# Finding and fetching the tokens of a rank one rank further ahead, ahead of the second product

## The chip, the cores and the metric

The kernel runs on one core of a Trainium2 chip. The metric is the device time of one execution in microseconds (us), as the median of several runs. Engines are named as the profile names them: PE (TensorE, matmuls and transposes; PEld is its weight load), DVE (VectorE), ACT (ScalarE), POOL (GpSimd, which also issues the indirect DMAs), SP (SyncE, which issues the weight loads).

## The reference, cut to what matters

One layer of a trunk for 512 prompt tokens and 8 sample tokens (520 rows, width 1024). After attention, a state space branch and a first layer norm comes a mixture of 64 experts, 8 for each token; this part is what the change touches.

```python
scores = sigmoid(xf @ w_router)
_, top_idx = top_k(scores + router_bias, 8)
gates = top_s / sum(top_s) * 2.5
# for every expert e, over the tokens tok that chose it, with gate g:
xb = x_pad[tok]
h = silu(xb @ w1[e]) * (xb @ w3[e])          # 1024 -> 256, twice
acc = acc.at[tok].add((h @ w2[e]) * g)       # 256 -> 1024
# and a shared expert for all tokens, then a second layer norm
```

## The kernel before, in words

The first 440 us compute everything up to the router. There the experts are sorted by how many tokens chose them; the position in this order is called the rank, 0 to 63, and rank e has a fixed capacity `CAPS[e]` (112 rows for the first, 56 for the last). Then the loop of `second_phase` (L1602) goes over the ranks. What one rank needs, by the names of the functions:

- `find(e)` (L1383): five small matmuls on PE (`x<-what,oh`) and three short DVE operations turn the one-hot table `oh` into the list of token numbers, `idx`, and the gates. PE writes into the one bank `x` (pool `psx`), which the side work uses too.
- `gather(e)` (L1412): POOL issues an indirect DMA that reads the listed rows of `xD` in memory into `XG[e % 3]`. There are three such buffers (`xg0` to `xg2`), so a gather must wait until the rank three before it has been turned.
- `turn(e)` (L1418): eight PE transposes of `xg` (`a<-ident,xg`), then ACT and DVE split the result into a high and a low part, `xgh` and `xgl`.
- `expert_in(e)`: the first product, 24 matmuls of 512 columns (`a<-hi,xgh`, `a<-lo,xgh`, `a<-hi,xgl`), over four chunks of weights; `ffn_mid` makes `hg` of it (ACT, DVE), and `ffn_turn(e)` transposes `hg` on PE and splits it into `hh` and `hl`.
- `expert_out(e)`: the second product, 12 matmuls (`mm<-hi,hh` and so on) over two chunks of weights; ACT scales it by the gate into `y`, and POOL issues a scatter, an indirect DMA that adds the rows of `y` to `accD` in memory.

The weights stream in the order of their use: for rank e+1 the four chunks of its first product, then the two chunks of the second product of rank e. Each chunk (512 KB) is loaded by SP into one of 7 raw buffers (5 more at the beginning), then split by ACT (`hi<-raw`) and DVE (`lo<-raw`) into one of 5 pairs of tiles; the `lo` of the first chunk of a second product is made by POOL, so POOL has, per rank, a gather, a scatter and one `lo`. Side work (the shared expert and the inputs of the layer, `x<-ph,...`) is spread over the ranks.

Step e of the loop issues: first product of e, turn of e+1, second product of e-1, `ffn_turn` of e, and then find and gather of e+3. This is the order in which the program is written; a scheduler then places the instructions of each engine, and may pull one ahead of others where it has its operands early by its own account. Each engine executes its instructions strictly in the placed order.

Of the kernel before, what the change touches and what calls it, by code (L numbers as in the profile page):

```python
# [31 lines left out]
NE = 64  # L32
# [168 lines left out]
def trunk_step(ctx: ExitStack, tc: tile.TileContext, I, O):  # L201
# [1074 lines left out]
    def shared_mid(out, hg):  # L1276
        S.activation(hg, out[:, 0:128], AF.Silu)
        mul(V, hg, hg, out[:, 128:256])
        return hg
# [128 lines left out]
    def fetch(e):  # L1408
        find(e)
        gather(e)  # L1410

    def gather(e):  # L1412
        m = CAPS[e]
        G.indirect_dma_start(out=XG[e % 3][0:m], out_offset=None, in_=xD[:, :],  # L1414
                             in_offset=bass.IndirectOffsetOnAxis(ap=IX[e][0:m, 0:1], axis=0),
                             bounds_check=NT - 1, oob_is_err=False)
# [60 lines left out]
    def second_phase():  # L1477
# [124 lines left out]
        for e in range(NE + 1):  # L1602
            if e == NE - 1:
                last_rows()
            if 0 < e < NE:
                expert_in(e)
            if 0 < e < NE - 1:
                turn(e + 1)
            if e:
                expert_out(e - 1)  # L1610
            else:
                H['shared'] = py.tile([128, 5, 2, 2, TT], F32R, tag="side", name="st")
                mids = py.tile([MAX_CAP, 1024], F32, tag="y", bufs=YB, name="mids")
                mids = [shared_mid(H['first half'][i], mids[0:TT, 128 * i:128 * i + 128]) for i in R5]
            if 0 < e < 6:
                shared_turn(mids[e - 1], e - 1, 0)
            if 0 < e < NE - 1:
                HT[e] = ffn_turn(HG.pop(e), CAPS[e])
            if e + 3 < NE:
                fetch(e + 3)  # L1620
            for i in {SECOND + 2: (0, 1, 2), SECOND + 3: (3, 4)}.get(e, ()):
                second_sums(i)
            if e == 4:
                close_pool(pre)
                pw = open_pool("pw")
            while side and (e - 4) * SIDE >= N_SIDE - len(side) + 1:
                q, i = side.pop(0)
                if q == -2:
                    shared_more(i)
                elif q == -1:  # L1630
                    shared_out(i)
                elif q < 4:
                    layer_inputs(q, i)
                else:
                    last_scales(i)
# [219 lines left out]
```

## Time and profile before

| | us |
|---|---|
| median of 3 runs (1320.13 to 1326.46) | 1321.36 |
| profiled execution, its own time | 1323.58 |
| its span, first to last instruction | 1321.8 |

The profile is one execution. The loop over the ranks fills it from about 440 to 1290 us. In the views used below a time is us from the start of the span; an idle time in brackets is how long the engine did nothing before that instruction, and what came last of what it waited for.

### The profile page before, as it was taken

What the parts mean: (1) busy time and instruction counts of PE and PEld (TensorE: products, weight loads), DVE (VectorE), ACT (ScalarE), POOL (GpSimd) and SP (SyncE); (2) the same over time, 40 slices, a digit from 0 to 9 for tenths busy, and PEclk for the clock granted to TensorE, in tenths of its full rate; (3) what the DMA queues carried; (4) which work ended last, traced back from release to release, by engine and by line L of the source; (5) the groups of instructions that cost most, each with busy time, mean ns of one, the idle gap of its engine ahead of it and who ended that gap; (6) DMA issues with size and microseconds to landing.
All of it is one profiled execution on the core that took longest, in us unless ns stands there. A gap on an engine that the chain in (4) does not pass through costs nothing. (4 is left out here: it accounts for less than half of the span.)

```text
span 1321.8 us, 20417 instructions
## 1 busy us (share of the span) xinstructions
PE 1182.6 (89%) x7082; PEld 884.3 (67%) x7084; DVE 933.0 (71%) x1440; ACT 702.9 (53%) x1055; POOL 459.2 (35%) x285
## 2 busy tenths in 40 slices
PE   6899999999997969888799888899899999988783
PEld 6899899899876846566566566677666666644341
DVE  7965658643487768576779666787878887766566
ACT  3232434233213656566567556677757767666463
POOL 1000000000012346343555335454555455465326
PEclk8899799999998879889999889999999999999897
DMA  9446553252523789889989978999999999979973
GB/s 367 158 135 167 198 162 129 72 155 83 180 77 106 246 217 274 254 263 304 296 254 314 290 237 278 285 329 314 321 311 313 335 314 299 303 249 289 260 230 97
DMA packets 112315, 312.92 MB, mean 237 GB/s; under 512 B 35121, under 2 KB 35545, under 8 KB 111135
## 3 DMA queue, kind: packets, MB, share of 16 engines
q1 hardware_dynamic: 78408, 261.74, 58.8%
q0 software_dynamic: 30848, 43.33, 14.8%
q10 hardware_dynamic: 2953, 6.52, 1.8%
q8 instruction: 57, 0.93, 0.3%
q14 instruction: 49, 0.40, 0.1%
HBM read 276.32 MB, written 32.87 MB: 234 GB/s over the span
## 5 line engine op out<-in xcount | busy, mean ns | idle before, releaser
L265 DVE TENSOR_TENSOR lo<-raw,hi 128x1024 fp32r<-128x1024 f32 x371 | 503.2, 1367 | 203.4 <-ACT hi L269 202.2
L269 ACT ACTIVATE hi<-raw 128x1024 fp32r<-128x1024 f32 x434 | 450.8, 1056 | 279.3 <-DMA raw<-in_we_dram 115.8
L210 PE MATMUL a<-hi,xgh 128*64 128x512 f32 (+18 forms) x512 | 212.3, 415 | 8.5 <-ACT hi L269 6.2
L1451 POOL DMA_INDIRECT accD<-y,idx x62 | 123.2, 1988 | 277.8 <-ACT hh L269 155.6
L210 PE MATMUL a<-lo,xgh 128*64 128x512 f32 (+18 forms) x512 | 210.9, 412 | 6.6 <-DVE lo L265 6.3
L210 PE MATMUL a<-hi,xgl 128*64 128x512 f32 (+18 forms) x512 | 207.0, 404 | 0.0
L265 POOL TENSOR_TENSOR lo<-raw,hi 128x1024 fp32r<-128x1024 f32 x63 | 168.3, 2672 | 62.5 <-ACT hi L269 51.8
L1414 POOL DMA_INDIRECT xg<-xD,idx x64 | 119.0, 1859 | 120.8 <-DVE idx L1396 57.9
L210 PE MATMUL mm<-xh,hi 128*128 128x260 f32 (+2 forms) x576 | 121.3, 292 | 16.6 <-ACT xh L269 6.6
L210 PE MATMUL mm<-xh,lo 128*128 128x260 f32 (+1 forms) x576 | 120.1, 290 | 1.8 <-DVE lo L265 1.8
L210 PE MATMUL mm<-xl,hi 128*128 128x260 f32 (+1 forms) x576 | 120.7, 291 | 0.8 <-DVE xl L265 0.8
L210 PEld LDWEIGHTS a<-hi,xgh 128*64 128x64 f32 (+18 forms) x512 | 75.7, 148 | 53.1 <-ACT hi L269 10.2
L210 PEld LDWEIGHTS a<-lo,xgh 128*64 128x64 f32 (+18 forms) x512 | 75.7, 148 | 45.4 <-DVE lo L265 10.7
L210 PEld LDWEIGHTS mm<-xh,hi 128*128 128x128 f32 x576 | 92.1, 195 | 17.5 <-ACT xh L269 6.3
L210 PEld LDWEIGHTS a<-hi,xgl 128*64 128x64 f32 (+18 forms) x512 | 75.7, 148 | 38.5 <-issue 4.3
L210 PE MATMUL mm<-lo,hh 128*64 128x512 f32 (+18 forms) x256 | 85.5, 416 | 12.8 <-POOL lo L265 9.9
L210 PEld LDWEIGHTS mm<-xh,lo 128*128 128x128 f32 x576 | 92.3, 195 | 2.1 <-DVE lo L265 2.0
L210 PEld LDWEIGHTS mm<-xl,hi 128*128 128x128 f32 x576 | 92.3, 195 | 1.5 <-DVE xl L265 1.1
L210 PE MATMUL mm<-hi,hh 128*64 128x512 f32 (+18 forms) x256 | 85.7, 417 | 8.0 <-ACT hi L269 7.6
L1450 ACT ACTIVATE y<-mm,both 78x1024 f32<-78x1024 f32 (+19 forms) x62 | 68.6, 1106 | 32.9 <-PE mm L210 29.8
L269 ACT ACTIVATE xgh<-a 128x256 fp32r<-128x256 f32 (+17 forms) x128 | 51.0, 408 | 63.7 <-PE a L215 63.0
L215 PEld LDWEIGHTS a<-ident,xg 64*128 64x128 f32 (+18 forms) x512 | 51.1, 147 | 48.9 <-issue 20.0
(410 smaller groups left out, 1919.4 us busy)
## 6 DMA issues: line engine op xcount, KB each, us to landing
raw<-in_we_dram SPq DMA_DIRECT2D x384, 512.0 KB
raw<-in_wd_dram SPq DMA_DIRECT2D x50, 512.0 KB
accD<-zeros_b POOLq DMA_DIRECT2D x2, 2560.0 KB, 23.7
praw<-in_wp_dram SPq DMA_DIRECT2D x8, 512.0 KB
base<-in_xtok_dram ACTq DMA_DIRECT2D x1, 2080.0 KB
xD<-base SPq DMA_DIRECT2D x5, 416.0 KB
base<-accD POOLq DMA_DIRECT2D x5, 416.0 KB, 22.8
acc<-accD SPq DMA_DIRECT2D x5, 416.0 KB
```

The costliest lines, as they stand in the source:

```text
L210: ins = nc.tensor.matmul(*a, **k)
L215: ins = nc.tensor.transpose(*a, **k)
L265: return e.tensor_tensor(out=o, in0=a, in1=b, op=ALU.subtract)
L269: a = S.activation(hi, src, AF.Copy)
L1414: G.indirect_dma_start(out=XG[e % 3][0:m], out_offset=None, in_=xD[:, :], in_offset=bass.IndirectOffsetOnAxis(ap=IX[e][0:m, 0:1], axis=0), ...
L1450: S.activation(y.rearrange("p (h n) -> p h n", h=2), ps[0:m], AF.Copy, scale=GC.pop(e)[0:m])
L1451: G.indirect_dma_start(out=sumsD[e % 2 if e < SECOND else 0][:, :], out_offset=bass.IndirectOffsetOnAxis(ap=IX.pop(e)[0:m, 0:1], axis=0), ...
```

## The change

In step e the find and the gather are now those of rank e+4 in place of e+3, and they stand between the turn of rank e+1 and the second product of rank e-1 in place of at the step's end. At step 0 ranks 3 and 4 are fetched together. The number of every kind of instruction stays the same; there are still three `XG` buffers, so the gather of rank e+4 goes into the buffer that the turn of rank e+1 has just read.

```diff
             if 0 < e < NE - 1:
                 turn(e + 1)
+            if e and e + 4 < NE:
+                fetch(e + 4)
             if e:
                 expert_out(e - 1)
...
             if 0 < e < NE - 1:
                 HT[e] = ffn_turn(HG.pop(e), CAPS[e])
-            if e + 3 < NE:
-                fetch(e + 3)
+            if e == 0:
+                fetch(3)
+                fetch(4)
```

Since the scheduler places instructions, the diff alone does not show where they come to stand. Three places follow.

POOL, around the gathers of ranks 15 to 17 (an `accD` row is a scatter, a `lo` row the split of a weight chunk, an `xg` row a gather). Before: gather 15, scatter 11, lo, scatter 12, lo, gather 16, gather 17, scatter 13.

```order
L1414 DMA xg0_4199<-xD_146,idx_6224 78x1024
L1451 DMA accD1_148<-y_6204,idx_5644 640x1024
L265 TENSOR_TENSOR lo_6287<-raw_6125,hi_6286 128x1024
L1451 DMA accD0_147<-y_6357,idx_5797 640x1024
L265 TENSOR_TENSOR lo_6408<-raw_6278,hi_6407 128x1024
L1414 DMA xg1_4201<-xD_146,idx_6377 78x1024
L1414 DMA xg2_4203<-xD_146,idx_6498 78x1024
L1451 DMA accD1_148<-y_6478,idx_5918 640x1024
```

Now, in the same engine and place: gather 15, scatter 10, lo, gather 16, scatter 11, lo, gather 17, scatter 12.

```order
L1414 DMA xg0_4199<-xD_146,idx_6051 78x1024
L1451 DMA accD0_147<-y_6081,idx_5340 640x1024
L265 TENSOR_TENSOR lo_6149<-raw_5987,hi_6148 128x1024
L1414 DMA xg1_4201<-xD_146,idx_6204 78x1024
L1451 DMA accD1_148<-y_6234,idx_5471 640x1024
L265 TENSOR_TENSOR lo_6302<-raw_6140,hi_6301 128x1024
L1414 DMA xg2_4203<-xD_146,idx_6357 78x1024
L1451 DMA accD0_147<-y_6387,idx_5624 640x1024
```

The gather of rank 16 has moved ahead of two scatters and two splits. From rank 9 on nearly every rank now has the pattern gather, scatter, lo, in which the gather of rank k stands just ahead of the scatter of rank k-5; before, the gathers of ranks 11, 12, 14 to 18, 40, 43, 44, 47 to 52 and 54 to 60 stood one or two scatters later than that, and most others there already. The gathers of ranks 23, 24, 25, 28 and 29 come to stand one scatter later than before.

POOL, at the beginning of the loop (scatter 0, lo, gather 4, then what follows).

```order
L1451 DMA accD0_147<-y_4724,idx_4298 640x1024
L265 TENSOR_TENSOR lo_4779<-raw_4467,hi_4778 128x1024
L1414 DMA xg1_4201<-xD_146,idx_4748 94x1024
L1451 DMA accD1_148<-y_4847,idx_4316 640x1024
L1414 DMA xg2_4203<-xD_146,idx_4871 92x1024
```

Those were the rows before; these are the rows now.

```order
L1451 DMA accD0_147<-y_4754,idx_4298 640x1024
L265 TENSOR_TENSOR lo_4794<-raw_4467,hi_4793 128x1024
L1414 DMA xg1_4201<-xD_146,idx_4638 94x1024
L1414 DMA xg2_4203<-xD_146,idx_4721 92x1024
L1451 DMA accD1_148<-y_4877,idx_4316 640x1024
```

The gather of rank 4 has what it had in front of it; the gather of rank 5 now stands ahead of the scatter of rank 1.

PE, between the transposes of `hg` of rank 8 (86 columns) and the first product of rank 9 (84 rows). Before, with the second product of rank 7 (88 rows) ahead of it:

```order
L210 MATMUL mm<-lo,hh 88x512 x2
L210 MATMUL mm<-hi,hl 88x512 x2
L215 MATMUL a<-ident,hg 128x86 x2
L215 MATMUL a<-ident,sg 128x104
L210 MATMUL a<-hi,xgh 84x512
```

Now (`x` rows are side work of the shared expert; behind the transposes of `hg` of rank 8 come eleven of them, of which the last three are shown):

```order
L210 MATMUL x<-ph,x1h 104x256
L210 MATMUL x<-pl,x1h 104x256
L210 MATMUL x<-ph,x1l 104x256
L210 MATMUL mm<-hi,hh 86x512 x2
L215 MATMUL a<-ident,sg 128x104
L210 MATMUL a<-hi,xgh 84x512
```

Side work has moved behind the transposes, and the first two matmuls of rank 8's second product now stand ahead of the whole first product of rank 9. The same is so at ranks 10, 11 and 12, and nowhere before the change.

## Rows read from the trace of the kernel before

**Rows 1.** Waits, 465:1290 us: who waited for what, total us, times, longest us.

```profile
ACT hi L269 <- DMA raw<-in_we_dram: 115.8, 83, 3.6
...
POOL xg L1414 <- PE a L215: 27.7, 13, 4.8
...
PE a L215 <- DMA xg<-xD,idx: 21.3, 4, 10.5
```

**Rows 2.** Windows: length, busy us of PE, PEld, DVE, ACT, POOL; clock, DMA share, GB/s.

```profile
440.00:860.00 420.00, 362.07 (x1931) 253.15 (x1930) 303.39 (x414) 259.44 (x360) 189.00 (x88) 0.93 0.88 270
860.00:1160.00 300.00, 292.59 (x1691) 194.88 (x1690) 244.37 (x332) 215.58 (x299) 151.43 (x74) 1.00 0.99 315
```

**Rows 3.** Timeline of PE: start us, us, instruction, [idle before <- releaser]; turns 4, 16, 56.

```profile
489.33 1.49 PE L215 MATMUL a<-ident,xg 94*128 94x94 f32 x8 [10.49 <-DMA xg<-xD,idx]
...
659.58 1.30 PE L215 MATMUL a<-ident,xg 78*128 78x78 f32 x8 [5.81 <-DMA xg<-xD,idx]
...
1171.22 0.68 PE L215 MATMUL a<-ident,xg 60*128 60x60 f32 x4 [4.07 <-DMA xg<-xD,idx]
```

**Rows 4.** Windows at and after these three waits, columns as in rows 2.

```profile
482.00:496.00 14.00, 6.67 (x29) 5.31 (x30) 4.60 (x10) 3.29 (x5) 1.06 (x1) 0.53 0.52 138
...
659.00:666.00 7.00, 6.42 (x27) 4.57 (x28) 2.47 (x5) 3.56 (x5) 0.00 (x0) 0.51 0.49 165
...
671.00:735.00 64.00, 59.93 (x318) 39.18 (x316) 52.43 (x76) 42.72 (x58) 37.01 (x17) 1.00 0.97 308
...
1170.00:1175.00 5.00, 3.78 (x15) 2.12 (x15) 3.28 (x3) 1.46 (x3) 2.65 (x2) 0.66 0.72 211
1175.00:1205.00 30.00, 30.00 (x150) 15.28 (x148) 20.81 (x32) 20.88 (x31) 17.06 (x9) 1.00 0.89 274
```

**Rows 5.** Timeline of DVE and POOL before gather 16 (scatter 11, idx 16, gather 16).

```profile
623.32 1.49 POOL L1451 DMA_INDIRECT accD<-y,idx  x1 [6.57 <-ACT sg L1277]
...
635.01 0.20 DVE L1396 TENSOR_SCALAR idx<-both,slots 78x1 int32<-78x1 f32 x1
...
640.01 1.80 POOL L1414 DMA_INDIRECT xg<-xD,idx  x1 [0.20 <-issue]
```

**Rows 6.** Timeline of POOL, scatter 51 and gather 56.

```profile
1139.47 1.44 POOL L1451 DMA_INDIRECT accD<-y,idx  x1 [0.30 <-PE a L210]
...
1154.63 1.23 POOL L1414 DMA_INDIRECT xg<-xD,idx  x1 [0.30 <-issue]
```

**Rows 7.** Tile xg, us from issue to landing: all 64 gathers; gather 4; gather 6.

```profile
DMA to landing us min/median/max: 6.7/12.0/24.4
...
DMA to landing us min/median/max: 22.0/22.0/22.0
...
DMA to landing us min/median/max: 9.2/9.2/9.2
```

**Rows 8.** Timeline of POOL after scatter 0: lo, gather 4, scatter 1, gather 6.

```profile
464.09 2.94 POOL L265 TENSOR_TENSOR lo<-raw,hi 128x1024 fp32r<-128x1024 f32 x1
467.23 2.35 POOL L1414 DMA_INDIRECT xg<-xD,idx  x1 [0.20 <-issue]
474.12 1.83 POOL L1451 DMA_INDIRECT accD<-y,idx  x1 [4.54 <-ACT y L1450]
...
484.45 1.06 POOL L1414 DMA_INDIRECT xg<-xD,idx  x1 [3.57 <-DVE idx L1396]
```

**Rows 9.** Timeline, PE and ACT: first product 9 begins, chunk splits, second product 8 begins.

```profile
567.64 0.73 PE L210 MATMUL a<-hi,xgh 128*84 128x512 f32 x1
...
569.30 2.95 ACT L269 ACTIVATE hi<-raw 128x1024 fp32r<-128x1024 f32 x3
...
577.03 0.68 PE L210 MATMUL mm<-hi,hh 128*86 128x512 f32 x2
```

**Rows 10.** Timeline of PE: first product of rank 21 begins; turn of rank 24.

```profile
726.41 0.43 PE L210 MATMUL a<-hi,xgh 128*76 128x512 f32 x1
...
758.67 0.42 PE L215 MATMUL a<-ident,xg 74*128 74x74 f32 x4
```

## Prediction

> **What bounds the kernel now.** I read the waits over the loop first, then the windows, then the timeline at the places that they name. The waits say how often PE stood still for a gather: 21.3 us, in four waits, the longest 10.5 us [rows 1]. That is the pool from which this change can draw. The same view shows a second limit beside it: ACT waited 115.8 us, in 83 pieces, for weight chunks to land [rows 1]. The windows put the two together. From 440 to 860 us PE is busy 362 of 420 us at a mean clock of 0.93, and the DMA engines are busy 0.88 of the time; from 860 to 1160 us PE is busy 292.6 of 300 us at full clock with the DMA share at 0.99 [rows 2]. So the loop has two nearly equal limits, PE and the weight stream. A stall that goes gives PE its time back, but only as much of it stays as the weight stream can follow.
>
> The timeline finds the three larger waits: before the turns of ranks 4 (10.49 us), 16 (5.81) and 56 (4.07) [rows 3]; the fourth, 0.9 us, is what is left of the 21.3. Each has a second price. In the window at rank 4 the granted clock is 0.53, at rank 16 it is 0.51, at rank 56 it is 0.66 [rows 4], that is, PE stood still, fell from 2.4 to 1.2 GHz, and worked on at the lower level. At rank 16 that is 7 us at 0.51, so 7 x 0.49 = 3.4 us more; at rank 56 it is 5 x 0.34 = 1.7 us more; at rank 4 it is 14 x 0.47 = 6.6 us more.
>
> **The change part by part.** Nothing is added: the same five find matmuls, DVE operations and gathers run per rank. What counts is where they stand.
>
> *Rank 16.* Its list was ready at 635.01 us, and POOL issued the gather only at 640.01, behind two scatters and two splits [rows 5]. PE wanted it at 653.8 (659.58 less 5.81) [rows 3]. In the new order the gather stands ahead of scatter 11, which ran at 623.32 [rows 5], and its find directly behind the turn of rank 13, ahead of the second product whose rows that scatter takes. So it is issued by about 623 us, 17 us sooner. Even with the longest landing of all 64 gathers, 24.4 us [rows 7], it is there at 648, 6 us before PE wants it. The wait goes. On PE this is worth 5.8 + 3.4 = 9.2 us. What the weight stream lets through is less: the DMA share in the window of the stall is 0.49, so the stall cost the stream 7 x 0.51 = 3.6 us, and the 64 us behind it run at a DMA share of 0.97 [rows 4]. Between 3.6 and 9.2 I take 5, near the lower end, because the stream is full in the stretch that follows.
>
> *Rank 56.* The gather was issued at 1154.63 us, and now stands ahead of scatter 51, which ran at 1139.47 [rows 6]: about 15 us sooner, against a wait of 4.07. The wait goes. On PE that is 4.1 + 1.7 = 5.8 us; by the DMA's idle time in that window alone, 5 x 0.28 = 1.4 us. Here the next 30 us have PE busy for all 30 with the DMA share at 0.89 [rows 4], so PE is what limits, and I take the upper end, 5.8.
>
> *Rank 4.* This is the largest wait, and I expect it to stay. The gather was issued at 467.23 directly behind a POOL split that began at 464.09 and took 2.94 us [rows 8]; its list was ready by then. The new order has the same scatter and the same split in front of it. It then took 22.0 us to land [rows 7]. What changes is behind it: gather 5 goes ahead of scatter 1. I put this at 0; the bounds are 17.1 us of gain (10.5 + 6.6, the wait gone) and, on the other side, a loss of some 2 us if gather 5 close behind it slows it (the nearest row is the 2.35 us for which a gather keeps POOL [rows 8]).
>
> A rule of the Trainium skill ("DMA: Bandwidth & Descriptors", section "Two DMAs through the same engine are not ordered") can be held against the trace here: within one queue of one DMA engine, descriptors start in order. By that rule nothing queued behind gather 4 can hold it, and the wait at rank 4 stays at 10.5 us. The rows read otherwise as easily: gather 6, issued 17 us after gather 4, landed 9.2 us later, at 493.7, while gather 4 landed at 489.2 [rows 7, 8], as if all that was outstanding drained together. By that reading a change behind gather 4 can matter, and the sum would lose up to the 17.1 us. No row decides, and this is one of the rivals.
>
> *POOL's queue.* A gather now waits in front of each scatter and each split. Before, 13 gathers waited for a turn to free their buffer, 27.7 us in all [rows 1], so that wait exists already, with the same work behind it. A gather blocks POOL 1 to 2.4 us [rows 6, 8]; behind it are the scatter, whose `y` has two buffers, and the `lo` of a chunk that PE wants one first product later. The cover is that product. I take 0; without cover it is the 2.4 us, in single ranks.
>
> *The pulled matmuls.* At ranks 8, 10, 11 and 12 the first two matmuls of the second product now stand ahead of the whole next first product. They need the first chunk of the second product, which comes fifth in the stream, behind the four chunks of the first product. At rank 8 the first product of rank 9 began at 567.64, and that fifth chunk was split second of the three in the ACT row that begins at 569.30, at 571.3 [rows 9]. So PE would begin 3.7 us later. Read the same way at the other three places the delay is 4.9, 3.6 and 1.6, together 13.8 us. But the first product of rank 9 took until 577.03, 9.4 us [rows 9], because its own chunks came one by one; begun later, it finds them all there and can end at the same time. So the price is between 0 and 13.8 us. I take 4, near the lower end for that reason.
>
> The sum: -5 - 5.8 + 4 = -6.8 us, on the profiled execution's 1323.58: 1316.8. The median of the runs lies 2.2 us below the profiled execution, so 1314.6 as a median. With all ends at their best it is -15.0 (1306.4), at their worst +13.8 - 3.6 - 1.4 = +8.8 (1330.2).
>
> **The rivals.** *B, slower: the pulled matmuls cost their full price.* If PE has no reserve at ranks 8 to 12, each delay is a real stall, and it takes the clock with it, as at rank 16 (3.4 us lost for 5.8 us stood, 0.6 per us): 13.8 x 1.6 = 22.1, less 10.8 for ranks 16 and 56, gives +11.3, 1332.7. It decides from an average of 1.7 us per place on (10.8 / 1.6 / 4). For it speaks that this stretch is where ACT waits for chunks; against it that a stall there also lets the stream run ahead.
>
> *C, no change: new waits for old.* Gathers 23, 24, 25, 28 and 29 come later than before. The find of rank 24 now stands in the middle of the first product of rank 21, which begins at 726.41; the turn of rank 24 is at 758.67 [rows 10]. That leaves some 28 us, and list, issue and the longest landing take about 3 + 24.4 [rows 7]. At the present pace it just fits. If PE gets faster there, ranks 24 and 25 wait, up to some 5 us each: -6.8 + 10 = +3.2, 1324.6.
>
> *D, much faster: the wait at rank 4 goes too*: -6.8 - 17.1 = -23.9, 1297.5. For it speaks the common landing; against it that the gather is issued no earlier.
>
> **How the numbers follow.** What a measurement of this kernel can tell from no change is about 0.5%, 6.6 us. The forecast has 0.52; its centre lies just beyond that bound, and I put 0.31 of it on faster and 0.21 on the same. B has 0.20 (slower), C 0.15 (same), D 0.13 (faster). So faster 0.44, same 0.36, slower 0.20. The range 1303 to 1331 holds the forecast with its bounds and C, and leaves out most of D and the upper part of B.
>
> **What would show it right or wrong.** In the profile after, the waits of PE on the gather should fall from 21.3 us to about 11, with one wait of 8 to 13 us before the turn of rank 4 and none at ranks 16 and 56; gather 16 issued ahead of scatter 11. The clock should stay at full from the turn of rank 9 through rank 20 where rank 16 broke it. The waits of ACT on chunks should grow by a few us behind rank 16: that is the part given back. B shows as idle time before `mm<-hi,hh` at ranks 8, 10, 11 and 12, C as new waits on `xg` at ranks 24 and 25, D as a gather 4 that lands within some 12 us. I am wrong altogether if the waits on the gather go and the time doesn't move: then the weight stream was the only limit.

## The result, and the profile after

The change made the kernel slower by 1.2%: 1339.01 us as the median of 4 runs (1337.28 to 1341.39), against 1322.88 us for the kernel before (4 runs); the ratio is 1.0116, 95% interval 1.0084 to 1.0147. The forecast was 1314.6 us with a range of 1303 to 1331; the time lies above it. The profiled execution of the changed kernel took 1339.84 us. Two executions further down (one each of kernels 8 and 9) ran in a slower state and are left out of the ratios, and the profile of kernel 8, which is of such an execution, is not used.

The waits over the loop, in the form of [rows 1] (who waited for what, total us, times, longest us; 465:1305 us, since the loop now ends later):

```profile
ACT hi L269 <- DMA raw<-in_we_dram: 113.7, 73, 4.8
...
POOL xg L1414 <- PE a L215: 47.4, 17, 6.6
...
PE mm L210 <- POOL lo L265: 24.4, 16, 4.6
...
PE a L215 <- DMA xg<-xD,idx: 12.4, 2, 6.3
...
PE mm L210 <- ACT hh L269: 7.1, 3, 5.0
```

PE's wait for gathers fell from 21.3 to 12.4 us, in two waits in place of four. A wait that the prediction set to nothing has taken its place: PE now stands 24.4 us for the `lo` that POOL makes. In the kernel before, that line (465:1290) reads 9.9 us:

```profile
PE mm L210 <- POOL lo L265: 9.9, 11, 1.6
```

POOL's gathers wait 47.4 us for a turn to free their buffer (27.7 before [rows 1]). That line is one of several: a gather also waits for its list, and some rows name another releaser. The pages have all of it in one row per kernel (busy us, mean ns of one, then the idle time of POOL in front of its gathers, and what ended most of it); here before, and then after:

```profile
L1414 POOL DMA_INDIRECT xg<-xD,idx x64 | 119.0, 1859 | 120.8 <-DVE idx L1396 57.9
```

```profile
L1414 POOL DMA_INDIRECT xg<-xD,idx x64 | 108.2, 1691 | 220.1 <-DVE idx L1396 47.4
```

So POOL stands 220.1 us in front of its gathers in place of 120.8.

The windows that answer to [rows 2], and two from the place looked at below:

```profile
440.00:860.00 420.00, 351.43 (x1835) 243.50 (x1834) 305.49 (x396) 252.56 (x350) 188.57 (x86) 0.91 0.87 262
860.00:1160.00 300.00, 293.00 (x1704) 197.90 (x1703) 245.15 (x331) 212.20 (x292) 148.06 (x75) 0.99 0.98 311
636.00:652.00 16.00, 11.27 (x49) 7.22 (x50) 14.84 (x19) 7.92 (x11) 12.05 (x4) 0.81 0.76 230
...
664.00:692.00 28.00, 19.46 (x69) 10.97 (x68) 13.17 (x20) 13.82 (x20) 5.95 (x4) 0.73 0.65 192
```

Most of the loss is in the first half of the loop: from 440 to 860 us PE is busy 351 us in place of 362, at a clock of 0.91 in place of 0.93. From 860 to 1160 us little has changed.

Now the single places. PE, in the timeline: the turns of ranks 4 and 25, and the second product of rank 8, which answer to [rows 3] and [rows 9].

```profile
483.55 1.49 PE L215 MATMUL a<-ident,xg 94*128 94x94 f32 x8 [6.08 <-DMA xg<-xD,idx]
...
566.91 0.69 PE L210 MATMUL mm<-hi,hh 128*86 128x512 f32 x2 [1.68 <-ACT hh L269]
...
787.20 0.73 PE L215 MATMUL a<-ident,xg 74*128 74x74 f32 x4 [6.34 <-DMA xg<-xD,idx]
```

The wait at rank 4 is 6.08 us (10.49 before), those at ranks 16 and 56 are gone, and rank 25 has a new one of 6.34, as rival C had it. The pulled matmul at rank 8 waits 1.68 us.

And POOL at the place where the longest of the new waits arises (gather 17, scatter 12, `lo` of the second product of rank 13); its first two rows are gather 16, now ahead of scatter 11, where [rows 5] has it 17 us behind:

```profile
622.62 2.03 POOL L1414 DMA_INDIRECT xg<-xD,idx  x1 [10.46 <-DVE xgl L265]
624.95 1.50 POOL L1451 DMA_INDIRECT accD<-y,idx  x1 [0.31 <-PE x L210]
...
636.50 2.00 POOL L1414 DMA_INDIRECT xg<-xD,idx  x1 [7.62 <-issue]
638.81 6.55 POOL L1451 DMA_INDIRECT accD<-y,idx  x1 [0.30 <-issue]
644.41 3.33 POOL L265 TENSOR_TENSOR lo<-raw,hi 128x1024 fp32r<-128x1024 f32 x1
```

The other engines at this place, in four views of the same timeline: DVE makes the list of gather 17, ACT the `y` of scatter 12 and the `hi` of the chunk, PE wants its `lo`, SP issues weight loads.

```profile
635.49 0.20 DVE L1396 TENSOR_SCALAR idx<-both,slots 78x1 int32<-78x1 f32 x1
```

```profile
634.52 1.11 ACT L1450 ACTIVATE y<-mm,both 82x1024 f32<-82x1024 f32 x1 [0.20 <-PE mm L210]
635.53 1.04 ACT L269 ACTIVATE hi<-raw 128x1024 fp32r<-128x1024 f32 x1
```

```profile
647.79 1.14 PE L210 MATMUL mm<-lo,hh 128*82 128x512 f32 x2 [4.59 <-POOL lo L265]
```

```profile
639.42 0.34 SPq L1315 DMA_DIRECT2D praw<-in_wp_dram  x1
647.77 3.57 SPq L318 DMA_DIRECT2D raw<-in_we_dram  x4
```

Read together: POOL stood 7.62 us in front of gather 17; the row names no releaser, but the last thing that the gather needed, its list, was written at 635.49 to 635.69. The scatter behind it had nothing left to wait for (0.30): its `y` was there at 635.63, so without the gather ahead it could have begun some 3 us earlier. `hi` was ready at 636.57 us, but `lo` began only at 644.41, 7.8 us late, and PE stood 4.59 us for it. Of these 7.8 us POOL spent 2.2 on gather 17 and 5.6 on the scatter, which is the longest of the 62 (6.55 us; the median is 1.84). Why it took so long no run shows; an estimate from these rows is that by its length alone, begun as soon as its `y` was there, `lo` would still have been 4.9 us late here. There is a second price. A raw buffer is free only when its `lo` is made, and SP executes in order: between 639.42 and 647.77 us no weight load was issued at all, and then four at once. The wait of SP for this `lo` was 7.8 us. The DMA share of 636:652 is 0.76. The bill comes two ranks later: from 664 to 692 us PE is busy 19.46 of 28 us at a clock of 0.73, and in this stretch ACT waits 13.9 us for chunks.

The whole loop can be summed up in the same way from POOL's timeline: the time in which a `hi` for POOL was ready and its `lo` had not begun is 65 us (51 before). For 41 of them POOL ran a scatter and for 14 a gather (22 and 18 before), and only for 2 it stood idle in front of a gather. So a gather that waits hardly holds `lo` back while it waits; what runs late behind its wait, the scatter above all, then falls into the time in which `hi` is ready.

The queue of SP shows its part over the whole loop (465:1290, what SP waited for, total us, times, longest us). Before:

```profile
SPq L318 <- POOL lo L265: 154.6, 51, 6.5
```

After:

```profile
SPq L318 <- POOL lo L265: 186.5, 58, 9.2
```

How the time of the loop divides can be worked out from the PE instructions: from the first matmul of rank 0's first product to the last second product, the time that PE stood, and of the time that it worked the part lost to the lower clock (for each piece of work, its length times one less its granted clock; where two matmuls overlap, the time counts once).

| | loop, us | PE stood | lost to the lower clock |
|---|---|---|---|
| before | 849.1 | 86.7 | 32.2 |
| after | 866.7 | 92.5 | 44.7 |

So of the 17.6 us 5.8 are more standing and 12.5 are more lost to the lower of the two clock levels while PE worked; the rest is -0.7. In total PE stands only a little longer. It stands at other places, and loses more by the clock.

### The profile page after: what moved, and what is told of

Read it like the earlier page. It is cut to its first block, busy times and chain, and to the rows that moved or that the text cites. A ratio compares the mean times of both kernels' runs of the same rounds, so it can differ in the third digit from the quotient of the medians.

```text
span 1338.0 us, 20409 instructions
## 1 busy us (share of the span) xinstructions
PE 1194.0 (89%) x7083; PEld 888.4 (66%) x7084; DVE 952.3 (71%) x1440; ACT 703.7 (53%) x1055; POOL 458.4 (34%) x285
## 5 line engine op out<-in xcount | busy, mean ns | idle before, releaser
L210 PE MATMUL a<-hi,xgh 128*64 128x512 f32 (+18 forms) x512 | 213.4, 417 | 5.5 <-ACT hi L269 3.6
L210 PE MATMUL a<-lo,xgh 128*64 128x512 f32 (+18 forms) x512 | 211.2, 412 | 3.6 <-DVE lo L265 3.6
L210 PE MATMUL a<-hi,xgl 128*64 128x512 f32 (+18 forms) x512 | 207.9, 406 | 0.0
L1451 POOL DMA_INDIRECT accD<-y,idx x62 | 134.0, 2162 | 198.2 <-ACT y L1450 95.2
L265 POOL TENSOR_TENSOR lo<-raw,hi 128x1024 fp32r<-128x1024 f32 x63 | 174.5, 2770 | 65.1 <-ACT hi L269 39.7
L1414 POOL DMA_INDIRECT xg<-xD,idx x64 | 108.2, 1691 | 220.1 <-DVE idx L1396 47.4
L210 PE MATMUL mm<-xh,hi 128*128 128x260 f32 (+2 forms) x576 | 121.9, 293 | 17.3 <-ACT xh L269 6.5
L210 PE MATMUL mm<-xl,hi 128*128 128x260 f32 (+1 forms) x576 | 120.8, 291 | 0.8 <-DVE xl L265 0.8
L210 PE MATMUL mm<-xh,lo 128*128 128x260 f32 (+1 forms) x576 | 120.2, 290 | 1.2 <-DVE lo L265 1.2
L210 PE MATMUL mm<-lo,hh 128*64 128x512 f32 (+18 forms) x256 | 87.5, 424 | 25.7 <-POOL lo L265 24.4
L210 PEld LDWEIGHTS a<-hi,xgh 128*64 128x64 f32 (+18 forms) x512 | 76.5, 149 | 50.3 <-ACT hi L269 6.3
L210 PEld LDWEIGHTS a<-lo,xgh 128*64 128x64 f32 (+18 forms) x512 | 76.4, 149 | 43.4 <-DVE lo L265 5.5
L210 PEld LDWEIGHTS mm<-xh,hi 128*128 128x128 f32 x576 | 92.7, 196 | 18.2 <-ACT xh L269 6.2
L210 PEld LDWEIGHTS a<-hi,xgl 128*64 128x64 f32 (+18 forms) x512 | 75.9, 148 | 41.5 <-issue 5.5
L210 PE MATMUL mm<-hi,hh 128*64 128x512 f32 (+18 forms) x256 | 88.1, 422 | 11.9 <-ACT hh L269 7.1
L210 PEld LDWEIGHTS mm<-xl,hi 128*128 128x128 f32 x576 | 92.5, 196 | 1.4 <-DVE xl L265 1.1
L210 PEld LDWEIGHTS mm<-xh,lo 128*128 128x128 f32 x576 | 92.2, 195 | 1.5 <-DVE lo L265 1.5
L210 PE MATMUL mm<-hi,hl 128*64 128x512 f32 (+18 forms) x256 | 85.5, 417 | 0.0
```

What stands on the lines that cost most here:

```text
L210: ins = nc.tensor.matmul(*a, **k)
L265: return e.tensor_tensor(out=o, in0=a, in1=b, op=ALU.subtract)
L1451: G.indirect_dma_start(out=sumsD[e % 2 if e < SECOND else 0][:, :], out_offset=bass.IndirectOffsetOnAxis(ap=IX.pop(e)[0:m, 0:1], axis=0), ...
```

## The experiments

Four theories went in. Theory 1: POOL's order; the gather now stands ahead of a scatter and of a `lo`, keeps both back since it waits for its list or its buffer, and PE and the weight stream wait for `lo`. Theory 2: the matmuls pulled ahead at ranks 8 to 12. Theory 3: the gathers of ranks 24 and 25, which come later. Theory 4: the weight stream limits whatever the order is. Each kernel was timed beside the kernel before; the table gives the median, the ratio to before with its 95% interval, and from the profile of each PE's waits on POOL's `lo` and on `xg` in the loop.

| | us | ratio | on lo | on xg |
|---|---|---|---|---|
| before | 1321 to 1323 | 1 | 9.9 | 21.3 |
| after | 1339.01 | 1.0116 (1.0084 to 1.0147) | 24.4 | 12.4 |
| 1 place only | 1336.16 | 1.0097 (1.0063 to 1.0132) | 16.8 | 24.1 |
| 2 rank only | 1327.64 | 1.0035 (1.0013 to 1.0057) | 16.0 | 6.4 |
| 3 no pull | 1343.98 | 1.0162 (1.0131 to 1.0192) | 23.4 | 12.5 |
| 4 gather behind lo | 1318.58 | 0.9975 (0.9952 to 0.9997) | 9.5 | 13.2 |
| 5 scatter behind lo | 1343.16 | 1.0143 (1.0110 to 1.0176) | 4.1 | 5.3 |
| 6 lo twice | 1418.35 | 1.0715 (1.0682 to 1.0749) | 72.2 | 3.9 |
| 7 two ranks | 1328.50 | 1.0039 (1.0013 to 1.0065) | 14.2 | 0.7 |
| 8 gather and scatter behind lo | 1335.40 | 1.0087 (1.0056 to 1.0117) | | |
| 9 six behind lo | 1326.24 | 1.0013 (0.9987 to 1.0038) | 10.2 | 9.3 |
| 10 six late | 1345.85 | 1.0171 (1.0138 to 1.0204) | 22.3 | 12.9 |
| 11 after, lo of the second chunk | 1326.40 | 1.0022 (0.9999 to 1.0045) | 16.3 | 8.5 |
| 12 as 4, lo of the second chunk | 1325.86 | 1.0024 (0.9997 to 1.0051) | 13.0 | 19.5 |
| 13 as 4, six early gathers late | 1320.24 | 0.9982 (0.9954 to 1.0010) | 12.5 | 18.1 |
| 14 as 4, six late gathers late | 1323.74 | 0.9998 (0.9972 to 1.0025) | 6.9 | 19.2 |

One warning for all of them: the scheduler places every instruction anew for each kernel, so none differs from its neighbour in one thing alone. That is why the cause below rests on runs in both directions, and not on one. And the waits are those of one execution: the profiles of rank only, 9 and 11 took 6 to 8 us less than the median of their kernel (1321.51, 1318.26 and 1318.00 us), so the waits of a median run may be longer, and that of 10 took 6 us more (1351.67).

### The two halves of the change

Place only (find and gather stay those of rank e+3):

```diff
+            if e and e + 3 < NE:
+                fetch(e + 3)
             if e:
                 expert_out(e - 1)
```

> Half of the change: find and gather stay those of rank e+3, and stand between the turn of rank e+1 and the second product of rank e-1. The matmuls pulled ahead at ranks 8, 10, 11 and 12 are the same as in the changed kernel. Theory 1 (POOL's queue: the gather now stands ahead of the scatter and of the lo split, keeps POOL while it waits for its list or its buffer, and PE then waits for lo): the place is what does that, so this kernel is slower than before too, 1330 to 1345 us, with PE's waits on lo well above the 9.9 us of before. Here the buffer is free earlier (the gather of e+3 takes the buffer that the turn of rank e has left), but the list is made just ahead, so the gather waits for its list. Theory 2 (pulled matmuls, 7.1 us of waits on hh): slower by 5 to 12 us, with waits on hh of some 5 to 9 us and lo near 10 us. Theory 3 (gathers 24 and 25 come later): the gather is one rank later than in the changed kernel, so several waits on xg in the ranks above 20, together more than 12 us. Theory 4 (the weight stream alone limits, any order loses as much as it wins): within 0.5% of before.

Rank only (those of rank e+4, at the old place):

```diff
-            if e + 3 < NE:
-                fetch(e + 3)
+            if e + 4 < NE:
+                fetch(e + 4)
```

> The other half: find and gather are those of rank e+4, at the old place behind the second product (ranks 3 and 4 fetched at step 0). The pulled matmuls are those of the changed kernel. Theory 1: the gather of rank e+4 waits for the turn of rank e+1, long done at this place, so POOL is not kept and PE's waits on lo stay near 10 us: within 0.5% of before or faster by up to 1%, 1308 to 1325 us, with the waits on xg at ranks 16 and 56 gone. Theory 2: slower by 5 to 12 us as the changed kernel, since the same matmuls are pulled: waits on hh 5 to 9 us. Theory 3: this place is half a rank later than in the changed kernel, so a wait at ranks 24 or 25 of 5 us or more again. Theory 4: within 0.5% of before.

Place alone costs 1.0%, rank alone 0.35%. Theory 1 said slower for the first, and that came; for the second it said within 0.5% and waits on `lo` near 10 us, and the waits are 16.0. Theory 4 wanted both near zero and falls for the place. But the waits on `lo` are nearly the same in both (16.8 and 16.0), and the place by itself also has more waits on `xg` than before, so this pair does not separate theories 1 and 3.

### The pulled matmuls undone

H['in'] is the first matmul of the next rank's first product:

```diff
+                    with tc.issue_after(H['in'].ins):
                         T.matmul(ps[0:m, h], lhsT=l[:, k], rhs=w[:, 512 * h:512 * h + 512], start=(k == 0 and n == 0),
```

> The changed kernel with one thing undone: the second product of a rank may not begin ahead of the first matmul of the next rank's first product, so that nothing is pulled ahead at ranks 8, 10, 11 and 12. Theory 2: the 7.1 us of waits on hh go, with the clock they cost some 10 us: 1327 to 1331 us. Theory 1 and theory 3: nothing to do with it, 1335 to 1341 us, the waits on lo still 20 to 28 us, the wait at rank 25 still 5 to 7 us. Theory 4: within 0.5% of the changed kernel.

Theory 2 falls: nothing is pulled ahead any more, and the kernel is not faster but, if anything, slower (1.0162 against 1.0116; the intervals overlap). The waits on `lo` stay at 23.4 us.

### The gather behind lo

```diff
+                if 1 < e < NE - 3:
+                    with tc.issue_after(H['lo of pool'].ins):
+                        gather(e + 3)
...
             if e and e + 4 < NE:
-                fetch(e + 4)
+                find(e + 4)
```

> The changed kernel with one thing undone: the find stays in its new place, a rank further ahead, but POOL issues the gather of a rank one step later, behind the lo split of that step (POOL's order is scatter, lo, gather). So a gather that waits stands behind the lo that PE wants, with about one rank less lead than in the changed kernel. Theory 1: PE's waits on lo fall from 24.4 us to 10 us or less and the time to 1318 to 1328 us. Theory 2: 1335 to 1341 us with waits on hh as in the changed kernel (about 7 us). Theory 3: later gathers mean more waits on xg, above 12 us: 1339 us or more. Theory 4: within 0.5% of the changed kernel.

This is the changed kernel but for the gather's place on POOL. The whole loss goes, and a little more: 1318.58 us, 0.9975 of before. The waits in its loop (465:1295), of which the first is now nearly empty:

```profile
POOL xg L1417 <- issue: 9.9, 54, 0.2
...
PE a L215 <- DMA xg<-xD,idx: 13.2, 6, 4.8
...
PE mm L210 <- POOL lo L265: 9.5, 10, 2.1
```

54 gathers find their list and their buffer ready (0.2 us each). The waits on `lo` are back at 9.5 us, and SP's longest wait on POOL's `lo` is 4.3 us in place of 9.2. The new find, a rank further ahead, stays where the change put it, so it is not the trouble. POOL stands 46.6 us in front of its 64 gathers, in place of 220.1, and the time in which `hi` was ready and `lo` had not begun is 38 us in place of 65: no gather runs in it, but scatters do, for 34 us.

```profile
L1417 POOL DMA_INDIRECT xg<-xD,idx x64 | 127.8, 1997 | 46.6 <-DVE idx L1399 34.2
```

### Only six ranks, in both directions

If a `lo` held back is the cause, a few ranks where it came late should carry much of it. Six were chosen: second products 9, 13, 17, 22, 27 and 37, whose `lo` came 1.3 to 7.8 us late. First the changed kernel with six gathers alone put behind `lo`:

```diff
+LATE = (10, 14, 18, 23, 28, 38)
...
+                if e in LATE:
+                    with tc.issue_after(H['lo of pool'].ins):
+                        gather(e + 3)
...
-                fetch(e + 4)
+                find(e + 4)
+                if e + 1 not in LATE:
+                    gather(e + 4)
```

> The changed kernel, with POOL's gather put behind the lo split at six ranks alone, those whose lo came 1.3 to 7.8 us late in the profile of the changed kernel (second products 9, 13, 17, 22, 27 and 37, so gathers 13, 17, 21, 26, 31 and 41); the other 50 gathers stay where the change put them. Theory 1 (a lo kept back by a waiting gather is what costs): these six hold 11 of the 24.4 us of waits on lo, so at 1.6 us of time for each us of wait (the rate from the kernel with every lo made twice: 100 us of time for 63 us of waits) some 17 us go: 1319 to 1327 us. Rival (no single ranks, the whole order decides): within 0.5% of the changed kernel, or a third of its loss.

1326.24 us: 12.8 of the 16 us come back from six gathers of the 59 that the change moved. POOL at the place shown above, `lo` of rank 13 and then gather 17:

```profile
632.54 2.46 POOL L1455 DMA_INDIRECT accD<-y,idx  x1 [6.62 <-ACT y L1454]
634.02 3.41 POOL L266 TENSOR_TENSOR lo<-raw,hi 128x1024 fp32r<-128x1024 f32 x1
637.62 6.05 POOL L1418 DMA_INDIRECT xg<-xD,idx  x1 [0.19 <-issue]
```

`lo` starts at 634.02 us, 10.4 us earlier than in the changed kernel and 1.0 us after its `hi`; the scatter in front of it takes 2.46 us in place of 6.55. The second product of rank 10 ends at 600.7 us in both profiles, that of rank 16 at 684.0 against 701.6 in the changed kernel, the last one at 1284.2 against 1304.3: most of what comes back comes back between ranks 10 and 16 (3.6 us of it by rank 11, where the pulled matmuls wait in the changed kernel).

Then the other way: the kernel with all gathers behind `lo`, and six of its splits made late, by making them three times over. The six are not quite those of the last run: `m` counts the chunks of weights, and `m // 6` is one more than the rank of the second product, so in the trace the splits made three times are those of ranks 8, 12, 16, 21, 26 and 36, and not 9, 13, 17, 22, 27 and 37 as the expectation has it.

```diff
+LATE = (9, 13, 17, 22, 27, 37)
...
+                    if m // 6 in LATE:
+                        for _ in range(2):
+                            H['lo of pool'] = sub(G, lo, raw, hi.bitcast(F32))
```

> The opposite dose: the kernel in which every gather stands behind lo (1318.6 us), with the lo of second products 9, 13, 17, 22, 27 and 37 made three times over, so that these six alone are some 5 to 6 us late, as they were in the changed kernel (up to 7.8). Theory 1: waits on lo rise by 10 to 20 us at these places and the time by 16 to 30 us, to 1333 to 1348. Rival (the six late splits were a symptom): below 1326 us.

1345.85 us, 27.3 more than without. The three longest waits of PE for `lo` in its profile (timeline; second products of ranks 13, 16 and 36):

```profile
650.91 1.15 PE L211 MATMUL mm<-lo,hh 128*82 128x512 f32 x2 [5.16 <-POOL lo L266]
...
707.03 1.14 PE L211 MATMUL mm<-lo,hh 128*78 128x512 f32 x2 [6.19 <-POOL lo L266]
...
978.80 1.12 PE L211 MATMUL mm<-lo,hh 128*68 128x512 f32 x2 [5.31 <-POOL lo L266]
```

Of the 22.3 us of waits 15.2 stand at ranks 12, 16, 26 and 36, whose split was made three times. The 5.16 us at rank 13 do not: its one split came late behind a scatter that took 8.73 us.

```profile
639.75 8.73 POOL L1458 DMA_INDIRECT accD<-y,idx  x1 [3.85 <-ACT y L1457]
647.52 3.33 POOL L266 TENSOR_TENSOR lo<-raw,hi 128x1024 fp32r<-128x1024 f32 x1
```

So a few late splits are enough for a loss of this size, at six ranks next to the six of the last run and not at the same ones, and mending six is enough to lose most of it. Theory 1 stands as far as the order on POOL goes. Long scatters have a part that is open: one of them makes up most of the delay at rank 13 in the changed kernel, and one makes `lo` late here by itself.

### Every lo twice

```diff
+                    H['lo of pool'] = sub(G, lo, raw, hi.bitcast(F32))
```

> The suspected cost made larger by itself, in the kernel in which the gather stands behind lo: POOL makes every lo twice, one subtraction right behind the other, so that each lo is ready some 2.4 to 3.4 us later; nothing else is added. Theory 1: PE's waits on lo rise from 9.5 us to 25 to 60, the low clock follows, and the time goes from 1318.6 to 1335 to 1360 us; the changed kernel with its mean lateness of lo 0.4 us above this one's lies inside that line. Rival, lo has cover enough (one first product, as the prediction had it): waits on lo below 15 us and at most 1325 us. Rival, the order placed by the scheduler elsewhere decides: no statement on lo, the waits grow in other lines.

1418.35 us, more than expected: 99.8 us for 62.7 us more of waits on `lo`.

```profile
PE mm L210 <- POOL lo L265: 72.2, 34, 5.4
```

The rates agree in size: 99.8 / 62.7 = 1.6 us of time for each us of wait here, 27.3 / 12.8 = 2.1 with six late, 20.4 / 14.9 = 1.4 between the changed kernel and the one with the gather behind `lo`. They are rough: the times are medians and the waits those of one execution each. With the times of the profiled executions they are 1.5, 2.6 and 1.5; with six gathers behind `lo`, by the medians, 12.8 / 14.2 = 0.9.

### The scatter behind lo

The indirect DMA of the second product becomes a function scatter(e, y), called one step later:

```diff
+        if 0 < e < NE - 4:
+            H['y'] = (e, y)
+        else:
+            scatter(e, y)
...
                 expert_in(e)
+                if 'y' in H:
+                    with tc.issue_after(H['lo of pool'].ins):
+                        scatter(*H.pop('y'))
```

> The changed kernel with POOL's queue turned round in another place: the gather stays where the change put it, and the scatter of a rank is issued behind the lo split that follows it (POOL's order is gather, lo, scatter in place of gather, scatter, lo). Theory 1 has two forms. If lo is late because it stands behind the gather and the scatter together, half of the delay goes: PE's waits on lo fall from 24.4 us to some 10 to 15, and the time to 1324 to 1332 us. If the waiting gather alone is enough, the waits on lo stay above 20 us and the time stays at 1336 to 1342. Rival, the scatter is the one that must not come late (it frees one of two y buffers, and ACT writes y behind each second product): waits of ACT y on the scatter appear, 1340 us or more. Rival, the loss has nothing to do with POOL's order: within 0.5% of the changed kernel.

```profile
POOL lo L265 <- ACT hi L269: 244.6, 41, 14.2
...
ACT y L1453 <- DMA accD<-y,idx: 86.5, 15, 9.7
...
PE mm L210 <- ACT hh L269: 14.1, 2, 9.5
...
PE mm L210 <- POOL lo L265: 4.1, 7, 1.1
```

The expected 1324 to 1332 us did not come (1343.16), though PE's waits on `lo` fell to 4.1 us. One rival had it: now POOL stands 244.6 us for `hi`, with the scatter behind it; the scatter frees one of the two `y`, so ACT stands 86.5 us in front of `y`, with `hh` and the next `hi` queued behind. It is the same kind of mistake in another place: here POOL's `lo` waits, and the scatter behind it is ready.

The same with the gather behind `lo` as well:

> The kernel with the gather behind lo, and the scatter behind lo as well: POOL's order is lo, scatter, gather, and nothing stands between a chunk's hi and its lo. Theory 1 with its price (the 9.5 us of waits on lo that are left, and the clock with them): 1308 to 1316 us, waits on lo below 6 us. Rival, the scatter comes too late for y: ACT y waits for it, 1320 us or more. Rival, what is left of the waits on lo comes from hi and not from POOL's queue: no difference from the kernel with the gather alone behind lo, 1316 to 1321 us.

1335.40 us, 17 more than with the gather alone behind `lo`. The time is that of the first rival; that it is `y` that is waited for is not shown here, since there are no rows.

### The lo of the second chunk

```diff
-                split(hi, lo, raw, G if 0 < m < 6 * (NE - 1) and m % 6 == 2 else V)
+                split(hi, lo, raw, G if 0 < m < 6 * (NE - 1) and m % 6 == 3 else V)
```

> The changed kernel, with POOL's lo split given the second chunk of a second product in place of the first (DVE makes the first). PE wants the second chunk six matmuls, some 2.6 us, later, so a lo that POOL makes late has that much more cover; gather and scatter keep their places on POOL. Theory 1: PE's waits on lo fall from 24.4 us to 5 to 12, time 1318 to 1330 us. Rival (a late scatter, or a late gather, is what costs): no gain, 1336 us or more. The list of later gathers (ranks 24, 25, 28, 29) stays, so waits on xg of some 6 to 12 us stay too.

The gather stays where the change put it, and PE wants POOL's `lo` six matmuls later. 12.6 us of the loss go, with 8.1 us less of waits on `lo` (16.3): the time is as expected, the waits fell by less. Together with the gather behind `lo` it brings nothing:

> Both together: every gather behind lo, and POOL's lo that of the second chunk. If the 9.5 us of waits on lo left in the kernel with the gather behind lo cost as much as the rest (1.6 us for each), 1304 to 1314 us, which would beat both kernels. Rival: those waits come from hi and the weight stream, not from POOL: 1316 to 1322 us. Rival: DVE, which now has the more urgent of the two splits, becomes late: waits on DVE's lo grow, 1322 us or more.

The waits on `lo` are 13.0 us there, not below 9.5, and the waits on `xg` 19.5; so the last 9.5 us could not be had in this way. The time, 1325.86 us, is that of the third rival, but not for its reason: PE's waits on DVE's `lo` are 2.5 us here and 3.8 with the gather alone behind `lo`. Why it is slower than that kernel stays open.

### What a wait for a gather is worth

The prediction priced the waits at ranks 16 and 56 at 10.8 us. Here the change is made for these two ranks alone, in the kernel before:

```diff
+EARLY = (16, 56)
...
+            if e + 4 in EARLY:
+                fetch(e + 4)
             if e:
                 expert_out(e - 1)
...
-            if e + 3 < NE:
+            if e + 3 < NE and e + 3 not in EARLY:
                 fetch(e + 3)
```

> The kernel before, with the change made for two ranks alone: find and gather of ranks 16 and 56 stand one rank further ahead and in front of the second product, all others where they were. This is the part of the prediction that dealt with ranks 16 and 56, by itself, and nothing is pulled ahead at ranks 8 to 12. The prediction's terms (5 and 5.8 us) give 10.8 us less: 1310 to 1313 us, waits on xg down to 11 us, one of 10 us at rank 4 left. Rival, the weight stream takes it back: the two waits go, the waits of ACT on chunks grow by as much, 1319 to 1324 us. Rival, POOL's queue takes it back: waits on lo rise by 3 us or more near ranks 12 and 52.

1328.50 us: not faster, but 0.4% slower. Its waits, as [rows 1] (one line was added at the top of this kernel, so L210 reads L211 here):

```profile
ACT hi L270 <- DMA raw<-in_we_dram: 138.6, 100, 4.4
...
PE mm L211 <- POOL lo L266: 14.2, 15, 1.6
PE a L211 <- ACT hi L270: 13.2, 11, 4.6
PE a L211 <- DVE lo L266: 9.5, 10, 4.1
PE a L216 <- DVE idx L1397: 5.5, 1, 5.5
...
PE a L216 <- DMA xg<-xD,idx: 0.7, 1, 0.7
```

The waits on `xg` are gone but for 0.7 us, and rank 4's, which stands here under `idx` with 5.5 us. In their place PE waits for the chunks of the first product (`hi` 13.2 and DVE's `lo` 9.5 us; 6.2 and 6.3 before), and ACT waits 138.6 us for chunks to land (115.8 before [rows 1]). PE stands 85.5 us in the loop in all, against 86.7. So the waiting has moved from the gather to the weights; both rivals, the stream and POOL's `lo` (up by 4.3 us), show in the waits; how much of the time each one took is not shown.

To price such a wait by itself, six gathers were made late in the kernel that has no `lo` trouble, once in the first half of the loop, once in the second:

```diff
+LATE = (13, 17, 21, 25, 29, 33)
...
-                if 1 < e < NE - 3:
-                    with tc.issue_after(H['lo of pool'].ins):
-                        gather(e + 3)
+                for k in (e + 2, e + 3):
+                    if 1 < e and 5 <= k < NE and (k in LATE) == (k == e + 2):
+                        with tc.issue_after(H['lo of pool'].ins):
+                            gather(k)
```

> What a wait of PE for a gather is worth, by itself: the kernel in which every gather stands behind lo (1318.6 us; PE's waits on the gather 13.2 us, on lo 9.5), with six gathers of the first half, those of ranks 13, 17, 21, 25, 29 and 33, put one more lo further back on POOL, so that they are issued some 12 to 14 us later; they still wait for nothing on POOL, so no lo is held. If a us that PE stands for a gather costs as much as a us that it stands for lo (1.6 to 2.1 us of time), 10 to 25 us of new waits on xg cost 16 to 50 us: 1335 to 1368. If the weight stream goes on meanwhile and gives most of it back (as the run with ranks 16 and 56 alone suggests, where 15 us of waits on xg went and the time did not fall), below 0.5 us for each: 1319 to 1330, with the waits of ACT on chunks smaller by about as much.

> The same with six gathers of the second half, ranks 37, 41, 45, 49, 53 and 57, where the DMA engines are busy 0.96 to 0.99 of the time. By the first reading (each us costs 1.6 or more) 1335 to 1360 here too; by the second the price is lower still than in the first half, since the stream has next to no idle time to lose: 1318 to 1326. If the stream is the limit here, the new waits on xg come with fewer waits on chunks behind them.

Two of the four new waits in the first half (ranks 17 and 25; ranks 21 and 29 have 2.1 and 5.7 us):

```profile
673.03 0.73 PE L216 MATMUL a<-ident,xg 78*128 78x78 f32 x8 [1.45 <-DMA xg<-xD,idx]
...
782.54 1.22 PE L216 MATMUL a<-ident,xg 74*128 74x74 f32 x8 [4.25 <-DMA xg<-xD,idx]
```

And the two in the second half (ranks 53 and 57):

```profile
1137.06 1.08 PE L216 MATMUL a<-ident,xg 62*128 62x62 f32 x8 [4.62 <-DMA xg<-xD,idx]
...
1191.46 1.11 PE L216 MATMUL a<-ident,xg 58*128 58x58 f32 x8 [5.62 <-DMA xg<-xD,idx]
```

By the ratios, 13.4 us of new waits in the first half cost (0.9982 - 0.9975) x 1322 = 0.9 us, and 10.2 us in the second half 3.0 us, each with some 4.8 us of uncertainty. At the lowest rate of a wait on `lo`, 1.4, they would have cost 19 and 14 us. Two of the six made no wait in the first half and four in the second, so the doses are small; and since other waits on `xg` fell, the total rose by only 4.9 and 6.0 us. Counted in that way the upper ends come to 1.2 and 1.3 us for each us, which is near the lowest rate of `lo`. The waits on `lo` moved as well, by as much as is to be measured: 12.5 us in the first and 6.9 in the second, against 9.5. At 1.4 that is 4.2 us more and 3.6 us less; with it taken out the new waits cost nothing in the first half and some 6.6 us in the second. That a wait for a gather is cheaper than one for `lo` is therefore likely for the first half, with the two-rank run beside it; for the second half, where it was expected to be cheaper still, these runs do not show it.

## Why the prediction was wrong, point by point

**POOL's queue, set to 0: the step that failed.** The prediction named what stands behind the gather (the scatter and `lo`), and gave two reasons for nothing: that the wait was there before, and that one first product covers `lo`. The first is true, but it read one line of that wait, and the wait grew from 27.7 to 47.4 us on turns and from 120.8 to 220.1 in all. The second was not borne out by the trace of before, where PE already stood 9.9 us for `lo` in 11 waits. And the bound of 2.4 us is the run of a gather alone: the scatter that is pushed back with it is left out. The delay was 7.8 us at rank 13, 2.2 for the gather and 5.6 for the scatter. What it cost in all is 14.5 us more of waits on `lo` (24.4 less 9.9), at 1.4 to 2.1 us each some 20 to 30 us, more than the whole loss, so the rate is rough. The term also forgot a customer of POOL: the raw buffer, and with it SP's queue and the weight stream.

**Ranks 16 and 56: the event right, the size wrong.** Gather 16 is issued at 622.62 us, gather 56 at 1151.03, and neither is waited for, as predicted. But the 10.8 us that this was to bring are not there when it is done alone (1328.50 us, interval 0.13% to 0.65% slower). The prediction had weighed the weight stream for rank 16 and taken the lower half; it should have taken nothing for both. The upper end at rank 56 rested on a window after the stall in which PE was busy throughout; that says who was busy, not who would have been late.

**Rank 4: 6.1 us, forecast 8 to 13.** Its bound of 17.1 us was too wide: the 6.6 us for the clock count the lower level while PE stood, too, and on the 6.67 us for which PE worked in that window [rows 4] it is 3.1. The wait fell though nothing in front of that gather moved. It is also 5.5 us in the two-rank kernel, whose POOL order around gather 4 is that of before, and 3.4 to 5.3 in the kernels of place only, rank only, no pull and gather behind `lo`. So the change is not what shortened it, and the 10.49 us of the profile of before [rows 3] may be a matter of that one execution; no run settles it. The prediction weighed the rule of the Trainium skill ("DMA: Bandwidth & Descriptors", section "Two DMAs through the same engine are not ordered") that descriptors within one queue start in order, against a common landing. The landing here changes (gather 4 issued at 465.61 us and its turn at 482.74 in the two-rank kernel, 17 us, against 22.0) with the same order behind it, so what stands behind gather 4 was not shown to matter, and no run speaks against the rule.

**The pulled matmuls, 4 of 0 to 13.8.** They do wait, 6.7 us in two places (1.68 at rank 8 and 5.03 at rank 11; the third wait of that line, 0.35 us at the loop's end, is there before too), though for `hh` and not for the chunk that the prediction looked at. Undone, the kernel is no faster. The lower end, 0, was right, and rival B falls as the cause, although its sign and its size (1332.7 us) were the nearest to the result; that they were is luck.

**Rival C, the gathers of ranks 24 and 25.** Rank 25 got its wait, 6.34 us. The kernels within 0.25% of before (4, 9, 11 to 14) have 8.5 to 19.5 us of waits on `xg` themselves, so such waits carry little of the loss.

**The sum.** -6.8 was forecast. With the term of POOL at 20 and those of ranks 16 and 56 and of the pulled matmuls at 0 it would have been +20 us; +16 was measured, but the 20 is taken from these runs and is no second measurement. The rival that was missing is the one that won: an instruction that waits, moved forward in an in-order queue, makes what stands behind it late.

A version that beats both kernels is the one with the gather behind `lo`: 1318.58 us, 0.9975 (0.9952 to 0.9997), some 3 us below before, an effect that lies below the 0.5% that one comparison can tell well.

## What to carry to other kernels

When an instruction that waits is moved forward in an in-order queue, price what is queued behind it by who waits for that, buffers and their refill included, and not only by how long the moved instruction itself takes: what stands between it and the late one is pushed back with it. The list can be moved ahead without the transfer that uses it. An instruction on a queue that is busy less than half of the time (POOL, 189 of 420 us from 440 to 860) can be expensive to delay. And before counting a stall as a gain, remove it alone: where two limits are nearly equal, the waiting moves to the other one.

## What the runs showed of the hardware

The price of a stall depends on what else stops with it. A us that PE stands for `lo` cost some 1.4 to 2.1 us of time by the three rates above, with a raw buffer held as well (at rank 13 no weight load was issued for 8 us); a us that PE stands for a gather cost less in the run that made such waits in the first half of the loop. And of the 17.6 us by which the loop grew, standing makes up 5.8 and work at the lower clock level 12.5: PE's granted clock was 0.81 in the window of the stall at rank 13 and 0.73 in the one that followed two ranks later.
